# New durations, and a port that two engines share, in the model behind a list scheduler: a two-block transformer kernel on one core

## The chip, the core and the metric

The kernel runs on one core of a Trainium2 chip. A core has five engines with a queue of instructions each, which run in the order in which they were issued: TensorE (PE in the profile, its weight loads PEld) for matrix products, VectorE (DVE), ScalarE (ACT) and GpSimd (POOL) for the rest, SyncE (SP) for issuing transfers. They meet through semaphores alone. The metric is the device time of one execution in microseconds (us).

## The reference

Two transformer blocks over 1024 tokens of width 1024, all in float32. What is cut here is what the argument doesn't touch.

```python
def first_block(x, c, ctx, ...):                # two layers
    for l in range(2):
        sh1, sc1, g1, sh2, sc2, g2 = split(silu(c) @ w_ada[l] + b_ada[l])
        hx = rmsnorm(x, g_pre_mix[l]) * (1 + sc1) + sh1
        q, k, v, u, gv, f = split(hx @ w_in[l])
        y = merge_heads(latent_window_attention(rope(q), rope(k), v, ck, cv, sink[l]),
                        spatial_gating(gelu(u), gelu(gv), ...), fourier_mix(f)) @ w_out[l]
        x = x + g1 * rmsnorm(y, g_post_mix[l])
        hx2 = rmsnorm(x, g_pre_ff[l]) * (1 + sc2) + sh2
        x = x + g2 * rmsnorm(square(relu(hx2 @ w_ff1[l])) @ w_ff2[l], g_post_ff[l])
    return x                                     # layer 0 runs the 256 context tokens too

def second_block(x, c, positions, ...):          # one layer
    h = rms_norm(x, g_mix) * (1 + sc_a) + sh_a
    cq, ckv, kr, dq, dk, dv = split(h @ w_in)
    mixed = concat(mla_attention(...), dilated_attention(...)) @ w_out
    x = x + gt_a * mixed
    h2 = rms_norm(x, g_ffn) * (1 + sc_m) + sh_m
    x = x + gt_m * expert_choice_ffn(h2, ...)    # 16 experts, each takes its 128 best tokens
    return rms_norm(x, g_final)
```

## The kernel before

**Tiling.** The tokens lie in tiles of 128. Matrix products run as two-part float32r products: an operand is split into a rounded high part (a copy) and the low part that is left (a subtraction), and a product is three passes (`mm3`) or two (`mm2`). So each block of weights of 128 x 1024 costs a load, a high copy on ScalarE or VectorE and a low subtraction on VectorE or GpSimd (`split`), and each result that becomes an operand again costs the same (`transpose_split`, `ev`, `expo`).

**What sets the order.** No line of the program says in which order the engines get their work. Each piece of work is a Python generator that yields where another may go ahead (`Task`); `Sched.run` picks, of those that may go on, the one of the best priority, and the instructions that it issues stand behind all earlier ones in their engines' queues. Whether a piece may go on is told by `Model`: a clock for each engine, moved on in `note` by an instruction's estimated cost after its inputs' estimated ends (`POST` and `PRE` are the estimated hand-over between engines). A task that needs an engine is held until that engine's clock is near. `copy`, `add` and `lo_any` also take the engine whose clock says that it will be through first, and `whole` lets a product run as one float32 product, without the split, where VectorE's clock is well behind TensorE's. The costs and clocks are numbers in Python; they set the order and the engine, and no time on the chip.

**Names used below.** The *first seam* is the step from layer 0's feed-forward to layer 1's projections, the *second seam* the one from layer 1's to the second block's. There `ff` ends, `finisher` makes the new residual and the next norm of each tile (`fin0` to `fin7`: `post`, `prenorm`, two times four transposes), and `passes` or `passes2` multiplies the tiles by the next weights (`proj`), which needs the first tile and four blocks of `w_in`, loaded and split by `Weights.task`. At the second seam `tables2` also makes tables of sines and cosines on VectorE. The *latent attention* is `mla_unit`, 16 units of 512 queries of a head: a first product for the maxima, a second for the scores, exponentials on ScalarE (`expo`), sums of them on GpSimd (`acc`), their split, and the product with the values. The *dilated attention* (`dil_unit`, 32 units) may run beside it and runs on behind it.

All engine calls go through `Engine.call`, so every instruction has one line, L186.

```python
    def lo_any(self, out, src, hi):
        n, c = size(out), self.m.clk
        if max(c["POOL"], self.m.now) + n * 0.0022 < max(c["DVE"], self.m.now) + n * 0.00104 + self.lbias:
            self.nc.gpsimd.tensor_sub(out, src, hi.bitcast(F32))
        else:
            self.lo(out, src, hi)
```

Of the kernel before, what the change touches and what calls it, by code (L numbers as in the profile page):

```python
# [38 lines left out]
PRE = 0.14  # L39
# [68 lines left out]
# ---------------------------------------------------------------- the order of the instructions  # L108
class Model:
    """What the instructions issued so far occupy: it decides which piece of work is issued next."""  # L110

    def __init__(self):
        self.clk = dict(PE=0.0, DVE=0.0, ACT=0.0, POOL=0.0, SP=0.0, DMA=0.0)
        self.cell, self.slot, self.last = {}, {}, {}
        self.events = []
        self.now = self.end = 0.0
        self.used = set()
# [11 lines left out]
    POST = dict(PE=0.25, DVE=0.2, ACT=0.15, POOL=0.1)  # L129

    def note(self, eng, cost, outs, ins, dma=False):
# [15 lines left out]
        else:  # L147
            e = self.clk[eng] = t + cost
# [13 lines left out]
def size(ap):  # L162
    n = 1
    for s in ap.shape[1:]:
        n *= s
    return n


class Engine:
# [3 lines left out]
    def __getattr__(self, op):  # L173
        f, m, name = getattr(self._r, op), self._m, self._n

        def call(*a, **k):
# [8 lines left out]
            m.note(eng, cost, outs, ins, "dma" in op)  # L185
# [4 lines left out]
    def cost(self, op, out, ins, k):  # L190
        n = max([size(out)] + [size(i) for i in ins])
# [5 lines left out]
        if e == "PE":  # L197
            if op == "transpose":
                return 0.109 if out.dtype == F32 else 0.056
            n = size(out)  # L200
            if ins[0].dtype == F32:
                return 2 * max(2 * n * 0.000417, 0.107)
            return max(n * 0.000421, 0.107)
        if e == "ACT":
            return 0.06 + n * 0.00083 + (0.09 if k.get("accum_out") is not None else 0)
        ps = any("PSUM" in str(i.space) for i in ins + [out])
        if e == "DVE":
            fast = op in ("tensor_copy", "tensor_scalar", "memset") and not ps and k.get("accum_out") is None
            return 0.07 + n * (0.00052 if fast else 0.00104)
        if op == "tensor_tensor" and k.get("op") == OP.pow:  # L210
            return 0.3 + 0.17 * n
        return 0.1 + n * 0.0022
# [7 lines left out]
class Sched:  # L220
# [16 lines left out]
    def run(self):  # L237
        """until all but the background is done"""
# [55 lines left out]
# ---------------------------------------------------------------- constants of the shapes  # L294
def rnd11(a):
    """float32 rounded to the 11 fraction bits of float32r"""
# [64 lines left out]
# ---------------------------------------------------------------- memory and arithmetic  # L361
class Base:
# [70 lines left out]
    def copy(self, out, src):  # L433
        """on whichever of the two engines is free first"""
# [22 lines left out]
    def mm2(self, out, v, hi, lo, start, stop):  # L457
        """v = [high | low] of 64 columns: the parts of the sum end up in the two halves of the rows"""
# [3 lines left out]
    def whole(self, t):  # L462
        """the vector engine is further behind than the tensor engine: a float32 product rather than two parts"""
# [3 lines left out]
    def fold(self, out, x):  # L467
        """x [high 64 | low 64, tokens] transposed, the halves added"""
# [14 lines left out]
    def bc_row(self, dst, row, n=1024):  # L483
        """every partition gets the row"""
# [16 lines left out]
    def lo_any(self, out, src, hi):  # L501
        """operands on chip: on whichever of the two engines is through first"""
# [7 lines left out]
class Reserve:  # L510
    """blocks kept back for a piece of work that has begun: it can always go on"""
# [32 lines left out]
class Weights:  # L544
    """Blocks of weights in the order of their use: loaded, then split in two float32r parts."""
# [71 lines left out]
class Block1(Base):  # L617
    # ---- start
# [29 lines left out]
    # ---- modulation  # L648
    def mod_pe(self, l, js, room):
        """both vectors of a layer on the tensor engine, 1024 columns at a time"""  # L650
# [33 lines left out]
    def mod_dve(self, l, js, wname, bname, wl, vecs):  # L684
        """weighted rows summed on the vector engine, then over the partitions on the tensor engine: 512 columns at a time"""
# [2722 lines left out]
```

## Time and profile before

| what | value |
|---|---|
| median of three runs | 4331.73 us (4331.38 to 4336.57) |
| span of the profiled execution (first to last instruction) | 4329.5 us |
| TensorE busy in it | 4034.2 us, 93% |
| VectorE, ScalarE, GpSimd busy | 64%, 42%, 18% |
| mean granted TensorE clock | 0.964 |

The profiled execution's own time outside the profiler is not recorded apart from its span; the median of the runs stands 2.2 us above the span. The span is read as TensorE's busy time plus its waits, since it has work or waits for work from the first product to the last. Its busy time is longer than its work, since in some stretches the granted clock is half of the full one.

### The profile page before, as it was taken

Reading aid. Unit: us, or ns where it says so; the run is one execution under the profiler, and the core shown is the slowest. Engines: PE = TensorE matmul, PEld = TensorE weight load, DVE = VectorE, ACT = ScalarE, POOL = GpSimd, SP = SyncE. Lnnn points to the kernel's source line nnn. Section 1 sums busy time; section 2 is a strip of 40 time slices with the busy share of each in tenths; the row PEclk is TensorE's granted clock in tenths of the full one; section 3 lists DMA queues with packets and bytes.
Section 4 is the critical chain, followed back from the end, with each engine's and each line's share of the span. In section 5 each row is a group of like instructions: output and inputs, shape, how many; then the busy total and the mean of one; then the engine's idle time right before and its main releaser. Section 6 shows DMA issues by size and latency. Waiting matters only on the chain. (4 is left out here: it accounts for less than half of the span.)

```text
span 4329.5 us, 54977 instructions
## 1 busy us (share of the span) xinstructions
PE 4034.2 (93%) x19984; PEld 3295.4 (76%) x19984; DVE 2780.2 (64%) x5030; ACT 1825.5 (42%) x3699; POOL 769.1 (18%) x853
## 2 busy tenths in 40 slices
PE   7998999999999979989999999798888898699997
PEld 3777778878887869878888888687676787587776
DVE  6447875666666385777233333814788776888898
ACT  3236643221221233564321222413455653687876
POOL 2111130000000061212000000401567424100001
PEclk8999999999999989999999999899889899799999
DMA  6202322233434240133111112423211345799998
GB/s 220 88 23 79 122 81 89 84 103 118 129 116 126 79 148 22 40 122 112 44 45 44 59 44 81 132 70 95 65 34 30 93 128 195 278 350 369 380 368 304
DMA packets 318761, 552.98 MB, mean 128 GB/s; under 512 B 93117, under 2 KB 177365, under 8 KB 318490
## 3 DMA queue, kind: packets, MB, share of 16 engines
q1 hardware_dynamic: 309130, 515.39, 34.9%
q0 software_dynamic: 9360, 34.08, 2.8%
q8 instruction: 157, 2.57, 0.2%
q14 instruction: 114, 0.93, 0.1%
HBM read 488.42 MB, written 60.97 MB: 127 GB/s over the span
## 5 line engine op out<-in xcount | busy, mean ns | idle before, releaser
L186 PE MATMUL ps<-blk 128*128 128x512 f32 (+3 forms) x16104 | 3542.5, 377 | 84.1 <-DVE blk L186 55.8
L186 PEld LDWEIGHTS ps<-blk 128*128 128x128 f32 (+1 forms) x16104 | 2847.1, 192 | 654.4 <-DVE blk L186 87.6
L186 DVE TENSOR_TENSOR blk<-blk 128x1024 fp32r<-128x1024 f32 (+7 forms) x808 | 922.9, 1182 | 139.1 <-ACT blk L186 126.0
L186 ACT CAST blk<-blk 128x1024 fp32r<-128x1024 f32 (+3 forms) x679 | 661.2, 1022 | 662.3 <-DMA blk<-in_w_ff_dram 390.3
L186 DVE TENSOR_TENSOR blk<-blk,ps 128x512 f32<-128x512 f32 (+1 forms) x488 | 324.8, 675 | 326.5 <-PE ps L186 324.9
L186 ACT CAST blk<-ps 128x512 fp32r<-128x512 f32 (+5 forms) x608 | 275.0, 480 | 441.7 <-PE ps L186 420.9
L186 PE MATMUL ps<-ident,blk 128*128 128x128 f32 (+1 forms) x2024 | 327.9, 296 | 113.6 <-DVE blk L186 53.4
L186 POOL TENSOR_TENSOR blk<-blk 128x1024 f32<-128x1024 f32 (+3 forms) x120 | 252.9, 2113 | 1004.4 <-DMA blk<-in_g_post_ff_dram 647.0
L186 DVE TENSOR_TENSOR blk<-ps,blk 128x512 fp32r<-128x512 f32 (+7 forms) x702 | 349.7, 532 | 108.9 <-ACT blk L186 83.1
L186 PEld LDWEIGHTS ps<-ident,blk 128*128 128x128 f32 x2024 | 261.8, 161 | 178.1 <-ACT blk L186 52.0
L186 ACT ACTIVATE hb<-ps 128x512 f32<-128x512 f32 (+2 forms) x194 | 106.5, 549 | 523.3 <-PE ps L186 512.5
L186 DVE SCALAR_TENSOR_TENSOR hb<-hb,cT 128x512 f32<-128x512 f32 x224 | 164.2, 749 | 112.5 <-DMA hb<-in_w_ada_dram 111.0
L186 ACT ACTIVATE blk<-blk,z 128x256 f32<-128x256 f32 (+2 forms) x406 | 214.4, 532 | 46.3 <-DVE z L186 41.3
L186 DVE CAST blk<-hb 128x512 fp32r<-128x512 f32 (+2 forms) x127 | 48.9, 389 | 262.6 <-ACT hb L186 258.0
L186 ACT ACTIVATE blk<-ps 128x512 f32<-128x512 f32 (+1 forms) x198 | 117.4, 598 | 187.6 <-PE ps L186 182.8
L186 ACT ACTIVATE hb<-hb 128x512 f32<-128x512 f32 (+5 forms) x386 | 176.1, 484 | 37.8 <-DVE hb L186 16.8
L186 ACT ACTIVATE blk<-blk 128x1024 f32<-128x1024 f32 (+4 forms) x157 | 117.4, 751 | 162.7 <-DVE blk L186 141.8
L186 ACT COPY blk<-ps 128x512 f32<-128x512 f32 (+2 forms) x131 | 77.2, 596 | 250.5 <-PE ps L186 250.4
L186 POOL TENSOR_TENSOR hb<-hb,blk 128x512 f32<-128x512 f32 x96 | 170.1, 1771 | 26.6 <-ACT blk L186 20.4
L186 DVE SCALAR_TENSOR_TENSOR blk<-blk,z 128x1024 f32<-128x1024 f32 (+2 forms) x146 | 155.0, 1095 | 21.1 <-POOL z L186 20.3
L186 DVE CAST blk<-ps 128x512 fp32r<-128x512 f32 (+2 forms) x178 | 93.5, 545 | 106.1 <-ACT blk L186 53.3
L186 POOL TENSOR_SCALAR sinkb<-sinkb 128x8 f32<-128x8 f32 x2 | 0.5, 245 | 888.8 <-DMA sinkb<-in_sink_dram 888.8
(150 smaller groups left out, 2060.6 us busy)
## 6 DMA issues: line engine op xcount, KB each, us to landing
blk<-in_w_ff_dram SPq DMA_DIRECT2D x128, 512.0 KB
blk<-in_w_gate_dram SPq DMA_DIRECT2D x128, 512.0 KB
blk<-in_w_up_dram SPq DMA_DIRECT2D x128, 512.0 KB
blk<-in_w_down_dram SPq DMA_DIRECT2D x128, 512.0 KB
hb<-in_w_ada_dram SPq DMA_DIRECT2D x208, 256.0 KB
blk<-in_w_ada_dram SPq DMA_DIRECT2D x40, 512.0 KB
blk<-in_w_in_dram SPq DMA_DIRECT2D x36, 512.0 KB
xd<-blk SPq DMA_DIRECT2D x32, 512.0 KB
```

The costliest lines, as they stand in the source:

```text
L186: return f(*a, **k)
```

## The change

It puts new numbers in `cost`, `POST` and `PRE`, and adds to `Model` the port that VectorE and GpSimd share: an instruction that `shares` marks starts, by the model, after the last marked one of the other engine. All other hunks take out comments and docstrings.

```diff
-PRE = 0.14
+PRE = 0.06
...
         self.cell, self.slot, self.last = {}, {}, {}
+        self.port = dict(DVE=0.0, POOL=0.0)
...
-    POST = dict(PE=0.25, DVE=0.2, ACT=0.15, POOL=0.1)
-
-    def note(self, eng, cost, outs, ins, dma=False):
+    POST = dict(PE=0.25, DVE=0.16, ACT=0.18, POOL=0.12)
+
+    def note(self, eng, cost, outs, ins, dma=False, shared=False):
...
         else:
+            if shared:
+                t = max(t, self.port["DVE" if eng == "POOL" else "POOL"])
+                self.port[eng] = t + cost
             e = self.clk[eng] = t + cost
...
-            m.note(eng, cost, outs, ins, "dma" in op)
+            m.note(eng, cost, outs, ins, "dma" in op, self.shares(op, out, ins))
...
         if e == "PE":
+            n = size(out)
             if op == "transpose":
-                return 0.109 if out.dtype == F32 else 0.056
-            n = size(out)
+                return 0.085 if ins[0].dtype == F32R else 0.112
+            if ins[0].dtype == F32R:
+                return max(n / 2400 + 0.0133, 0.06)
             if ins[0].dtype == F32:
-                return 2 * max(2 * n * 0.000417, 0.107)
-            return max(n * 0.000421, 0.107)
+                return 2 * max(2 * n / 2400 + 0.0025, 0.112)
+            return max(n / 2400 + 0.0025, 0.025)
+        ps = any("PSUM" in str(i.space) for i in ins + [out])
+        acc = k.get("accum_out") is not None
+        column = any(size(i) == 1 for i in ins)
         if e == "ACT":
-            return 0.06 + n * 0.00083 + (0.09 if k.get("accum_out") is not None else 0)
-        ps = any("PSUM" in str(i.space) for i in ins + [out])
+            return (0.06 if ps else 0.1) + n * 0.00083 + (0.1 if acc else 0) + (0.075 if column else 0)
         if e == "DVE":
-            fast = op in ("tensor_copy", "tensor_scalar", "memset") and not ps and k.get("accum_out") is None
-            return 0.07 + n * (0.00052 if fast else 0.00104)
+            fast = op in ("tensor_copy", "tensor_scalar", "memset") and not ps and not acc
+            return 0.07 + n * (0.00052 if fast else 0.00104) + (0.062 if op == "scalar_tensor_tensor" or fast and column else 0)
         if op == "tensor_tensor" and k.get("op") == OP.pow:
-            return 0.3 + 0.17 * n
-        return 0.1 + n * 0.0022
+            return 0.25 + 0.19 * n
+        return 0.2 + n * 0.0021
+
+    def shares(self, op, out, ins):
+
+        n = sum("PSUM" not in str(i.space) and size(i) > 1 for i in ins)
+        if self._n == "POOL":
+            return n > 0
+        return self._n == "DVE" and (n > 1 or n == 1 and op in ("tensor_copy", "tensor_scalar") and "PSUM" not in str(out.space))
```

The work is the same but for what the three choosers decide. Over the whole program VectorE issues 3 instructions more and ScalarE 29 fewer; GpSimd gets 7 more tensor-tensor instructions, among them 9 low parts of exponentials, 5 of queries and 3 of keys in the latent attention, all VectorE's before. In the dilated attention 19 products more run as one float32 product (13 of 256 columns, 6 of 128) in place of 38 float32r ones, and in the first block's attention 7 of 512 columns in place of 14.

The order changes all along the program. These are the places that the prediction speaks of. In each pair, the first rows are of before (L186) and the second of the change (L190).

At the second seam, TensorE's queue: `ident` marks the finisher's transposes, the long rows of `blk` alone are first the last of `ff` (multiples of 12 up to 24) and then `proj`.

```order
L186 MATMUL ps<-blk 128x512 x12
L186 MATMUL ps<-ident,blk 128x128 x4
L186 MATMUL ps<-blk 128x512 x24
L186 MATMUL ps<-ident,blk 128x128 x20
L186 MATMUL ps<-blk 128x512 x60
L186 MATMUL ps<-ident,blk 128x128 x4
```

```order
L190 MATMUL ps<-blk 128x512 x12
L190 MATMUL ps<-ident,blk 128x128 x4
L190 MATMUL ps<-blk 128x512 x12
L190 MATMUL ps<-ident,blk 128x128 x16
L190 MATMUL ps<-blk 128x512 x90
L190 MATMUL ps<-ident,blk 128x128 x4
L190 MATMUL ps<-blk 128x512 x30
L190 MATMUL ps<-ident,blk 128x128 x4
```

Before, the last rows of `ff` are followed by 20 transposes (of `fin4`, `fin5`, again both, and the first half of `fin6`) and then `proj`; now `proj` comes after 16 transposes, with 90 products ahead of the second half of `fin5` and 120 ahead of the first of `fin6`.

At the same place, SyncE's queue: `xd_93` is the finisher's store of a tile's residual, `in_w_in` a block of the next weights, `posi` and `inv` inputs of the tables.

```order
L186 DMA xd_93<-blk 128x1024
L186 DMA posi<-in_positions_dram 128x8x1
L186 DMA hb<-in_inv_dram 128x96
L186 DMA blk<-in_w_in_dram 128x2x512
L186 DMA xd_93<-blk 128x1024
L186 DMA blk<-in_w_in_dram 128x2x512 x2
L186 DMA blk<-in_positions_dram 128x1024
L186 DMA invT<-in_invT_dram 128x2
L186 DMA blk<-in_w_in_dram 128x2x512 x3
```

```order
L190 DMA xd_93<-blk 128x1024 x2
L190 DMA posi<-in_positions_dram 128x8x1
L190 DMA hb<-in_inv_dram 128x96
L190 DMA blk<-in_w_in_dram 128x2x512 x6
L190 DMA blk<-in_positions_dram 128x1024
L190 DMA invT<-in_invT_dram 128x2
L190 DMA xd_93<-blk 128x1024
```

Before, one block of weights stands ahead of the store of `fin6` and the fourth behind it and behind the inputs of the tables; now six stand together ahead of that store.

At the first seam, SyncE's queue: `xd_91` is the residual's store (in the first rows of `fin5`, `fin6` and `fin7` in turn, in the second of `fin4`, `fin5` and `fin6`; `xd_90` is a tile that is read).

```order
L186 DMA xd_91<-blk 128x1024
L186 DMA blk<-in_w_in_dram 128x2x512 x3
L186 DMA xd_91<-blk 128x1024
L186 DMA blk<-in_w_in_dram 128x2x512
L186 DMA xd_91<-blk 128x1024
L186 DMA blk<-in_w_in_dram 128x4x256 x4
```

```order
L190 DMA blk<-xd_90 128x1024
L190 DMA blk<-in_w_in_dram 128x2x512 x2
L190 DMA xd_91<-blk 128x1024
L190 DMA blk<-in_w_in_dram 128x2x512
L190 DMA xd_91<-blk 128x1024
L190 DMA blk<-in_w_in_dram 128x2x512
L190 DMA xd_91<-blk 128x1024
```

Before, three blocks of weights stand behind the store of `fin5` and the fourth behind that of `fin6`; now the fourth stands behind the store of `fin5`. On TensorE the first 12 products of `proj` stood behind all eight transposes of `fin5` and now stand ahead of them.

In the latent attention, GpSimd's queue: `hb<-blk` and `hb<-hb,blk` are the sums of exponentials (one unit has one and six), `MEMSET` belongs to the queries.

```order
L186 MEMSET blk 1x512
L186 TENSOR_TENSOR hb<-hb 32x512
L186 TENSOR_TENSOR blk<-hb,blk 96x512
L186 TENSOR_TENSOR hb<-blk 128x512
L186 TENSOR_TENSOR hb<-hb,blk 128x512 x6
```

```order
L190 TENSOR_TENSOR hb<-hb 32x512
L190 TENSOR_TENSOR hb<-blk 128x512
L190 TENSOR_TENSOR blk<-hb,blk 96x512
L190 TENSOR_TENSOR hb<-hb,blk 128x512 x6
L190 TENSOR_TENSOR blk<-blk 128x1024
```

Before, a unit's sums follow each other and no low part of 128 x 1024 is among them; now GpSimd also has such a subtraction (`blk<-blk 128x1024`) behind or between a unit's sums, at nine places of the stage.

## Rows read from the trace of the kernel before

**Rows 1.** The page: span, and busy time, share and instructions of each engine

```profile
span 4329.5 us, 54977 instructions
...
PE 4034.2 (93%) x19984; PEld 3295.4 (76%) x19984; DVE 2780.2 (64%) x5030; ACT 1825.5 (42%) x3699; POOL 769.1 (18%) x853
```

**Rows 2.** Stretches: length; PE, PEld, DVE, ACT, POOL busy (x); clock, DMA, GB/s

```profile
1554.00:1613.00 59.00, 36.64 (x169) 29.75 (x168) 58.56 (x61) 22.74 (x45) 45.34 (x42) 0.83 0.47 160
2100.00:2700.00 600.00, 600.00 (x2649) 496.81 (x2648) 189.29 (x255) 133.97 (x187) 2.40 (x1) 1.00 0.18 55
2709.00:2790.00 81.00, 54.30 (x247) 44.15 (x247) 75.05 (x102) 33.12 (x61) 43.78 (x40) 0.85 0.40 129
3020.00:3397.00 377.00, 319.75 (x1463) 251.46 (x1463) 304.53 (x443) 205.50 (x371) 243.12 (x152) 0.89 0.17 43
3400.00:3567.00 167.00, 156.11 (x1033) 141.25 (x1033) 135.82 (x396) 108.30 (x299) 50.38 (x28) 0.94 0.47 124
3800.00:4300.00 500.00, 489.13 (x2290) 395.07 (x2288) 447.41 (x479) 388.29 (x501) 37.85 (x25) 1.00 0.97 362
```

**Rows 3.** What TensorE waited for, whole span: us in total, times, longest

```profile
PE ps L186 <- DVE blk L186: 112.4, 82, 14.7
```

**Rows 4.** Timeline of the second seam: start, us, instruction, idle before

```profile
2745.99 0.40 SPq L186 DMA_DIRECT2D blk<-in_w_in_dram  x1
...
2752.79 0.33 SPq L186 DMA_DIRECT2D xd<-blk  x1
2753.28 1.19 SPq L186 DMA_DIRECT2D blk<-in_w_in_dram  x2
...
2755.66 13.35 SPq L186 DMA_DIRECT2D blk<-in_w_in_dram  x3
...
2756.31 2.82 PE L186 MATMUL ps<-ident,blk 128*128 128x128 f32 x12 [7.44 <-DVE blk L186]
...
2766.66 5.88 POOL L186 TENSOR_TENSOR blk<-blk 128x1024 f32<-128x1024 f32 x1 [8.34 <-DVE blk L186]
2767.39 2.36 DVE L186 TENSOR_TENSOR blk<-blk 128x1024 fp32r<-128x1024 f32 x2
...
2772.60 1.11 PE L186 MATMUL ps<-ident,blk 128*128 128x128 f32 x4 [13.47 <-POOL blk L186]
...
2773.36 16.09 PE L186 MATMUL ps<-blk 128*128 128x512 f32 x60
```

**Rows 5.** Timeline of the first seam

```profile
1592.68 1.83 SPq L186 DMA_DIRECT2D blk<-in_w_in_dram  x3
...
1598.69 0.34 SPq L186 DMA_DIRECT2D xd<-blk  x1
...
1599.14 0.37 SPq L186 DMA_DIRECT2D blk<-in_w_in_dram  x1
...
1604.56 3.48 DVE L186 TENSOR_TENSOR blk<-blk 128x1024 fp32r<-128x1024 f32 x3
...
1606.96 1.97 PE L186 MATMUL ps<-ident,blk 128*128 128x128 f32 x8 [14.66 <-DVE blk L186]
...
1608.58 4.03 PE L186 MATMUL ps<-blk 128*128 128x512 f32 x12
```

**Rows 6.** Timeline of the end of layer 0 attention

```profile
508.43 1.94 PE L186 MATMUL ps<-ident,blk 128*128 128x128 f32 x8 [3.92 <-DVE blk L186]
```

**Rows 7.** Groups of instructions: a plain float32 product of 512 columns

```profile
L186 PE MATMUL ps<-blk,cT 128*2 128x512 f32 x128 | 62.3, 623 | 6.3 <-DMA blk<-in_w_ada_dram 6.3
```

**Rows 8.** VectorE in 2100 to 2700 us, where GpSimd is idle

```profile
L186 DVE TENSOR_TENSOR blk<-blk 128x1024 fp32r<-128x1024 f32 x54 | 64.9, 1223 | 56.2 <-ACT blk L186 56.2
```

**Rows 9.** The latent attention, 3020 to 3397 us

```profile
L186 POOL TENSOR_TENSOR hb<-hb,blk 128x512 f32<-128x512 f32 x96 | 170.1, 1771 | 26.6 <-ACT blk L186 20.4
L186 DVE TENSOR_TENSOR blk<-blk 128x1024 fp32r<-128x1024 f32 x67 | 112.6, 1685 | 9.9 <-ACT blk L186 9.4
```

**Rows 10.** GpSimd over the whole span: its low parts of 128 x 1024

```profile
L186 POOL TENSOR_TENSOR blk<-blk 128x1024 fp32r<-128x1024 f32 x17 | 41.8, 2465 | 39.9 <-ACT blk L186 28.4 <-PE ps L186 8.9 <-DVE rden L186 1.5
```

## The prediction

> **What bounds the kernel now.** The page first: TensorE is busy for 4034 of the 4329.5 us of the span [rows 1]. With 93% on one engine, no order of the same products can give more than the waits that are left and what the low clock adds, so the question is where the waits lie. The table by stretches tells that. In the feed-forward TensorE waits for nothing (600 of 600 us), and in the experts it is busy for 489 of 500 us while the transfer engines are at 0.97: there a new order has nothing to win. It waits at the two seams (22 of 59 us at the first, 27 of 81 at the second) and in the latent attention (57 of 377 us), all with a granted clock of 0.83 to 0.89, where 1.00 is 2.4 GHz and the low level 1.2 [rows 2]. The table of waits says for whom: VectorE's blocks end 112 us of them [rows 3]. So I cost the change at those three places, and the float32 products that it adds by themselves.
>
> **Second seam: -11 us.** Before, `proj` starts at 2773.36, right behind the first transposes of `fin6`, for which TensorE waited 13.47 us: an addition on GpSimd that began at 2766.66 and took 5.88. Ahead of that lies a wait of 7.44 us for `fin5` and `fin4` [rows 4]. Now `proj` stands ahead of `fin6`, so what it waits for is its own: the fourth block of weights. Its load is the first of the three at 2755.66, and its low part is the first of the two from 2767.39, done at about 2768.6 (half of 2.36 us). So with the old loads `proj` could have begun 4.8 us sooner. But the loads move too: the blocks behind the first waited in SyncE's queue for the store of `fin6` at 2752.79, and now six stand ahead of it. At the pace of two in 1.19 us the fourth is issued some 2 us behind the first, at about 2748 in place of 2755.7, so 8 us sooner. Its low part now stands behind fewer instructions on VectorE as well: five low parts follow each other there, where before three were followed by a tile's transposes, its norm and a table, and then two. I take 6.6 of the 8 us on top of the 4.8: `proj` starts at about 2762. What is late next is `fin6`: it has 120 products ahead of it, 27 us at 0.2265 us each (600 us by 2649 [rows 2]), which reach to 2789, and its transposes were ready at 2772.6 before. Bounds: -4 (the order alone) and -13.5 (the whole wait); the 7.44 us stay.
>
> **First seam: -5 us.** Here `proj` starts at 1608.58, and the low part of its fourth block ends at 1608.04 (1604.56 and 3.48). So the wait of 14.66 us that is booked on `fin5` hides a wait for weights, and putting `proj` ahead of `fin5` alone gives nothing. The fourth load went out at 1599.14, right behind the store of `fin6` at 1598.69; now it stands behind the store of `fin5`, with which before the three loads from 1592.68 went out [rows 5]. At 0.6 us each that is about 1594.5, 4.6 us sooner, and `fin6` and `fin7` no longer stand ahead on VectorE. Bounds: 0 and -14.7.
>
> **End of layer 0's attention: -3 us.** The transposes of `front1` waited 3.92 us with nothing behind them [rows 6]; they now stand ahead of the last attention products, which fill the wait. Bounds: 0 and -3.9. In layer 1 the same is done to a shorter wait; I give it nothing.
>
> **Float32 products: +5 us.** The nearest row is a float32 product of 512 columns with two rows out: 128 records for 64 products, 62.3 us, so 0.97 us each [rows 7]. Two float32r products are 0.45 us, so 0.52 us more, and by the columns an estimated 0.26 at 256 and 0.13 at 128: 7 x 0.52 + 13 x 0.26 + 6 x 0.13 = 7.8 us of TensorE. Most are in the dilated attention, where TensorE is busy for 156 of 167 us [rows 2], so little is hidden; but each saves VectorE a split there. +5, bounds 0 and +7.8.
>
> **Latent attention: -5 us.** The port is plain in the rows: VectorE's subtraction of 128 x 1024 takes 1.223 us where GpSimd is idle [rows 8] and 1.685 us here, where GpSimd is busy for 243 of 377 us, 96 of its additions at 1.771 us each [rows 9]. The 67 of them lose 31 us that way, which the old model didn't count: it issued work that was not to be ready. Now four more units of the dilated attention (12 in place of 8) are through before the last latent unit, products that wait for nothing of this stage, and nine low parts of exponentials leave VectorE (9 x 1.685 = 15 us) for GpSimd, where one takes 2.465 us [rows 10], 22 us in all. VectorE at 304 of 377 us and GpSimd at 243 [rows 2] both have room, but a low part on GpSimd stands behind sums in its queue. I take a small gain, -5, with bounds of -28 (half of TensorE's 57 us) and +39 (below).
>
> A rule stands against this term: the Trainium skill, page "Perfetto Trace Analysis", section "Optimizing Scalar/DVE Operations", says that moving work between GpSimd and VectorE might not help, since they share a read port. By it the nine low parts free nothing and hold the port for longer, 9 x (2.465 - 1.223) = +11 us in place of -5; it gives the second rival below.
>
> **Everything else: 0.** The order changes in every stage, but the feed-forward has no waits to lose, pieces of attention and Fourier work only change places, and the routing is the same instructions on VectorE.
>
> Sum: -11 - 5 - 3 + 5 - 5 = -19, so a span of 4310.5 us. The profiled execution has 4329.5, and the median of the runs stands 2.2 us above it: **4313 us**.
>
> **Rivals.** *Slower: GpSimd is late in the latent attention.* Each of the nine low parts ends up to 2.465 + 2 x 1.771 - 1.685 = 4.3 us later than on VectorE, behind two sums, and the product with the values waits for it in TensorE's queue with all that stands behind: up to 39 us. For it speaks that TensorE's waits here are for VectorE most of all; against it that more dilated products stand between. It decides from 24 us on (the other terms are -14, and 10 more pass the measure); at three quarters, 29 us, the time is 4313 + 5 + 29 = 4347. *No change: the port eats the gain.* With +11 in the latent attention, as above, the sum is -11 - 5 - 3 + 5 + 11 = -3, 4329 us. For it speaks that both engines lose time to the port now; against it that VectorE's wait falls as well as GpSimd's rises. *Faster still:* half of the latent attention's 57 us go, -28 in place of -5: 4290 us. For it speaks that the old model was blind to the port just there; against it that VectorE has little spare time.
>
> **How the numbers follow.** The forecast 0.48, slower 0.20, no change 0.17, faster still 0.15. A measurement of this kernel tells about 0.2%, 8.7 us, from no change (4323 to 4340). Nearly all of the forecast's own range (4300 to 4328) and all of the last case are faster: 0.60. The rest of the forecast and most of the second rival are the same: 0.20. Slower: 0.20. The range leaves out the lower half of the last case and the upper half of the first rival: 4285 to 4345; the forecast's own is 4300 to 4328.
>
> **What would show it.** At the second seam the row with 60 products should be one with 90, starting some 11 us sooner by the end of `ff`, with no wait of 13 us ahead of it; at the first seam a wait of 9 to 10 us in place of 14.66. In the latent attention, a busy GpSimd above 0.65 of the stage, VectorE's subtractions still near 1.7 us, and TensorE's waits at 50 us or so. The experts should take the same time from their first product on. The prediction is wrong if waits appear where there are none now, in the attention of the first block above all, if TensorE's waits for GpSimd's blocks grow from stage to stage, or if the 57 us grow.

## The result: slower by 1.0%

The changed kernel takes 4380.66 us (median of 4 runs, 4375.11 to 4384.74), the kernel before 4334.15 beside it (4331.38 to 4343.10): ratio 1.0100, interval [1.0087, 1.0114]. The forecast was 4313, and the range ended at 4345. The profiled execution took 4380.09, its span is 4378.3.

The page answers to [rows 1]: TensorE is busy for 30 us more and the span is 49 us longer, so it waits 19 us more and also takes 30 us longer for its products, on the same number of records, at a mean granted clock of 0.959 (0.964 before).

```profile
span 4378.3 us, 54861 instructions
...
PE 4063.8 (93%) x19984; PEld 3315.3 (76%) x19984; DVE 2744.7 (63%) x5033; ACT 1827.5 (42%) x3662; POOL 791.1 (18%) x860
```

The table by stretches answers to [rows 2]: first seam, second seam, latent attention, experts.

```profile
1558.00:1617.00 59.00, 43.61 (x210) 35.27 (x210) 58.85 (x63) 24.75 (x52) 41.61 (x44) 0.88 0.40 134
2727.00:2808.00 81.00, 69.02 (x311) 55.94 (x310) 71.72 (x93) 34.84 (x68) 44.27 (x46) 0.92 0.39 132
...
3040.00:3449.00 409.00, 350.22 (x1648) 278.22 (x1646) 285.90 (x461) 237.43 (x438) 265.11 (x170) 0.89 0.18 43
3830.00:4330.00 500.00, 470.62 (x2208) 386.36 (x2207) 428.80 (x463) 377.85 (x492) 59.58 (x25) 0.97 0.97 358
```

Both seams gained, as forecast: 7 and 15 us more work in stretches of the same length. The experts, where TensorE was busy for 489 of 500 us, now have 471. The table of waits over the whole span says for whom; VectorE's row [rows 3] fell by half, and others grew, the gathered blocks of the experts (3.7 us before) most plainly:

```profile
PE ps L190 <- ACT blk L190: 64.0, 101, 3.6
PE ps L190 <- DVE blk L190: 58.3, 68, 3.3
PE ps L190 <- DVE hb L190: 44.8, 18, 22.7
PE ps L190 <- POOL blk L190: 42.4, 16, 12.6
PE ps L190 <- DMA blk<-h,idxT: 30.4, 7, 7.7
```

TensorE has the same number of records under the same names in both programs (a float32 product counts as two), so each stage can be timed from the start of its first product to that of the next stage's first. In us, from the two profiled executions:

| | stage | before | after | change |
|-|-|-|-|-|
| A | start, layer 0's attention and output projection | 639.6 | 654.7 | +15.1 |
| B | first feed-forward, seam, projections to the last key | 1074.9 | 1062.8 | -12.1 |
| C | layer 1's attention, with queries and Fourier work | 213.8 | 243.9 | +30.1 |
| D | output projection | 103.3 | 102.9 | -0.4 |
| E | second feed-forward and seam | 878.3 | 864.3 | -14.0 |
| F | rest of the projections, latent and dilated attention, output, routing | 806.5 | 814.5 | +7.9 |
| G | experts | 576.5 | 599.2 | +22.6 |
| H | final sum | 10.7 | 9.3 | -1.4 |

The sum is +47.8. The gains (B and E, 26 us) are larger than the 16 forecast; the losses lie in A, C and G, for which the forecast had -3 and twice zero, and in F (-5 and +5). By the table by stretches over each stage, TensorE's waiting changed by +2.5 us in A, -8.1 in B, +17.0 in C, -12.7 in E, +0.6 in F and +20.1 in G; the rest of each change is longer or shorter busy time. Stage A before and after, and in a third kernel that has the order of the kernel before on every engine up to the experts (`late_gather`, below):

```profile
5.09:644.67 639.58, 583.93 (x3086) 442.81 (x3086) 414.57 (x993) 282.87 (x825) 127.68 (x233) 0.97 0.30 103
5.12:659.78 654.66, 596.52 (x3085) 449.80 (x3085) 417.90 (x1004) 281.17 (x811) 117.59 (x228) 0.95 0.29 101
5.20:653.90 648.70, 590.46 (x3086) 448.18 (x3086) 415.80 (x993) 283.20 (x825) 125.07 (x233) 0.96 0.30 101
```

The first and the third row differ by 9 us with the same order, 6.5 of them busy time, so of A's 15 us as little as 6 may be the change's.

**The seams.** The timeline answers to [rows 4]. TensorE's waits ahead of the row of `proj` are 5.74 and 3.97 us in place of 7.44 and 13.47, and the row has 90 products:

```profile
2768.58 9.18 SPq L190 DMA_DIRECT2D xd<-blk  x2
2779.49 4.01 SPq L190 DMA_DIRECT2D blk<-in_w_in_dram  x6
...
2782.26 1.12 PE L190 MATMUL ps<-ident,blk 128*128 128x128 f32 x4 [5.74 <-POOL blk L190]
2787.35 1.97 PE L190 MATMUL ps<-ident,blk 128*128 128x128 f32 x8 [3.97 <-POOL blk L190]
2788.96 22.36 PE L190 MATMUL ps<-blk 128*128 128x512 f32 x90
...
2790.83 5.76 DVE L190 TENSOR_TENSOR blk<-blk 128x1024 fp32r<-128x1024 f32 x5
```

The last feed-forward product ends at 2775.9 here and at 2748.4 before, so `proj` begins 13 us behind it, where it was 25. It begins while five of the six low parts of its weights are still to be made (the last row), right behind the transposes. At the first seam the wait is 12.60 in place of 14.66 [rows 5]; 6 us of B's gain lie in smaller waits, most of them ahead of it, and 4 in shorter busy time:

```profile
1607.86 1.97 PE L190 MATMUL ps<-ident,blk 128*128 128x128 f32 x8 [12.60 <-POOL blk L190]
1609.48 3.86 PE L190 MATMUL ps<-blk 128*128 128x512 f32 x12
```

**The experts.** On GpSimd's queue, before, from the eighth expert on each gather is issued some 9.5 us behind a scatter and 24 to 27 us ahead of its transposes:

```profile
3960.64 1.59 POOL L186 DMA_INDIRECT xo<-blk,idxT  x1 [24.63 <-DVE blk L186]
3970.19 0.98 POOL L186 DMA_INDIRECT blk<-h,idxT  x1 [7.97 <-ACT blk L186]
3997.18 1.59 POOL L186 DMA_INDIRECT xo<-blk,idxT  x1 [26.00 <-DVE blk L186]
4006.73 0.98 POOL L186 DMA_INDIRECT blk<-h,idxT  x1 [7.97 <-DMA blk<-in_w_gate_dram]
```

After, gathers come in no rhythm, and TensorE stands in front of their transposes:

```profile
4071.80 1.72 POOL L190 DMA_INDIRECT blk<-h,idxT  x1 [0.30 <-PE ps L190]
4078.15 1.12 PE L190 MATMUL ps<-ident,blk 128*128 128x128 f32 x4 [4.81 <-DMA blk<-h,idxT]
...
4112.03 1.22 POOL L190 DMA_INDIRECT blk<-h,idxT  x1 [5.94 <-ACT blk L190]
4120.39 1.12 PE L190 MATMUL ps<-ident,blk 128*128 128x128 f32 x4 [6.75 <-DMA blk<-h,idxT]
```

From a gather's issue to its first transpose, experts 3 to 15, worked out from such rows: before 18.8 to 28.5 us and no wait; after 7.2, 8.0, 12.6, 10.2, 17.3, 10.8, 29.5, 6.3, 8.4, 14.9, 5.6, 9.0 and 16.6. Six of these waited; for them (5.6 to 10.2) it is the time that the block took to arrive.

**Layer 1's attention.** In the order of the program before, the 124 products of its Fourier work stand between attention products almost to the end. After, they stand in one piece of some 40 us (1795 to 1834), together with the last queries; the attention from the third tile on comes behind it, alone. The stage before and then after:

```profile
1719.50:1933.40 213.90, 197.60 (x1230) 169.78 (x1227) 171.15 (x520) 132.24 (x407) 43.47 (x95) 0.98 0.25 82
```

```profile
1722.60:1966.50 243.90, 210.61 (x1228) 172.64 (x1227) 175.87 (x537) 130.53 (x389) 43.55 (x97) 0.96 0.21 72
```

TensorE waits for 33 us in this stage where it waited for 16, and is busy for 13 us longer at a granted clock of 0.96 in place of 0.98.

### The profile page after: what moved, and what is told of

Read it like the earlier page. It is cut to its first block, busy times and chain, and to the rows that moved or that the text cites. A ratio compares the mean times of both kernels' runs of the same rounds, so it can differ in the third digit from the quotient of the medians.

```text
span 4378.3 us, 54861 instructions
## 1 busy us (share of the span) xinstructions
PE 4063.8 (93%) x19984; PEld 3315.3 (76%) x19984; DVE 2744.7 (63%) x5033; ACT 1827.5 (42%) x3662; POOL 791.1 (18%) x860
## 5 line engine op out<-in xcount | busy, mean ns | idle before, releaser
L190 PE MATMUL ps<-blk 128*128 128x512 f32 (+6 forms) x16104 | 3556.6, 379 | 87.4 <-DVE blk L190 38.9
L190 PEld LDWEIGHTS ps<-blk 128*128 128x128 f32 (+2 forms) x16104 | 2862.3, 193 | 657.2 <-DVE blk L190 62.8
L190 DVE TENSOR_TENSOR blk<-blk 128x1024 fp32r<-128x1024 f32 (+8 forms) x806 | 909.1, 1167 | 237.9 <-ACT blk L190 228.0
L190 ACT CAST blk<-blk 128x1024 fp32r<-128x1024 f32 (+3 forms) x696 | 678.0, 1021 | 665.3 <-DMA blk<-in_w_ff_dram 365.7
L190 DVE TENSOR_TENSOR blk<-blk,ps 128x512 f32<-128x512 f32 (+1 forms) x488 | 322.7, 676 | 316.8 <-PE ps L190 315.8
L190 ACT CAST blk<-ps 128x512 fp32r<-128x512 f32 (+4 forms) x553 | 256.6, 487 | 531.6 <-PE ps L190 505.7
L190 POOL TENSOR_TENSOR blk<-blk 128x1024 f32<-128x1024 f32 (+4 forms) x122 | 261.6, 2150 | 966.8 <-PE ps L190 667.9
L190 PE MATMUL ps<-ident,blk 128*128 128x128 f32 (+1 forms) x2024 | 329.0, 296 | 106.9 <-POOL blk L190 32.5
L190 DVE TENSOR_TENSOR blk<-ps,blk 128x512 fp32r<-128x512 f32 (+7 forms) x687 | 340.9, 530 | 120.6 <-ACT blk L190 100.9
L190 PEld LDWEIGHTS ps<-ident,blk 128*128 128x128 f32 x2024 | 261.6, 160 | 178.7 <-ACT blk L190 55.9
L190 ACT ACTIVATE hb<-ps 128x512 f32<-128x512 f32 (+2 forms) x194 | 106.6, 549 | 524.5 <-PE ps L190 512.4
L190 DVE SCALAR_TENSOR_TENSOR hb<-hb,cT 128x512 f32<-128x512 f32 x224 | 165.5, 754 | 127.0 <-DMA hb<-in_w_ada_dram 125.5
L190 DVE CAST blk<-hb 128x512 fp32r<-128x512 f32 (+2 forms) x129 | 51.6, 402 | 282.5 <-ACT hb L190 278.0
L190 ACT ACTIVATE blk<-blk,z 128x256 f32<-128x256 f32 (+2 forms) x406 | 214.3, 532 | 32.1 <-DVE z L190 31.9
L190 ACT COPY blk<-ps 128x512 f32<-128x512 f32 (+2 forms) x155 | 91.9, 603 | 269.8 <-PE ps L190 269.3
L190 DVE CAST blk<-ps 128x512 fp32r<-128x512 f32 (+2 forms) x218 | 108.9, 515 | 136.5 <-ACT blk L190 70.1
L190 ACT ACTIVATE hb<-hb 128x512 f32<-128x512 f32 (+3 forms) x378 | 174.1, 488 | 24.8 <-DVE blk L190 9.5
L190 ACT ACTIVATE blk<-ps 128x512 f32<-128x512 f32 (+1 forms) x198 | 116.9, 599 | 157.5 <-PE ps L190 152.1
L190 ACT ACTIVATE blk<-blk 128x1024 f32<-128x1024 f32 (+4 forms) x157 | 117.4, 751 | 149.8 <-DVE blk L190 136.6
L190 DVE SCALAR_TENSOR_TENSOR blk<-blk,z 128x1024 f32<-128x1024 f32 (+2 forms) x146 | 158.8, 1120 | 18.6 <-POOL z L190 18.5
L190 POOL TENSOR_TENSOR hb<-hb,blk 128x512 f32<-128x512 f32 x96 | 156.5, 1632 | 33.3 <-ACT blk L190 28.0
L190 POOL TENSOR_SCALAR sinkb<-sinkb 128x8 f32<-128x8 f32 x2 | 0.5, 246 | 885.1 <-DMA sinkb<-in_sink_dram 885.1
```

Source lines behind the costliest of these rows:

```text
L190: return f(*a, **k)
```

## The experiments

Theory from these rows: the losses are separate accidents of order, each in its place: a gather that is issued late, Fourier work that is not there when the attention waits, and something at the end of layer 0's attention. Main rival: the port in the model, or a slower chain of VectorE, ScalarE and GpSimd, costs in all stages alike. The gaps of a gather "in the model's time" in the expectations are between its issue and its transposes by the scheduler's own clock. The numbers by stage against before, from one profiled execution each (ahead of the first difference in order, stage A differed by up to 9 us between executions, the others by 4, so less is not read):

| kernel | A | B | C | E | F | G | ratio to before |
|-|-|-|-|-|-|-|-|
| after | +15 | -12 | +30 | -14 | +8 | +23 | 1.0100 [1.0087, 1.0114] |
| `act_only` | +1 | 0 | -5 | -2 | +9 | +4 | 0.9996 [0.9986, 1.0005] |
| `late_fourier` | +15 | -10 | +3 | -14 | +6 | +20 | 1.0045 [1.0028, 1.0062] |
| `early_gather` | +15 | -10 | +30 | -16 | +6 | +4 | 1.0060 [1.0038, 1.0083] |
| `no_port` | +11 | -3 | -5 | -1 | -2 | +50 | 1.0123 [1.0106, 1.0139] |
| `both` | +13 | -9 | +3 | -14 | +9 | +8 | 1.0026 [1.0016, 1.0035] |
| `port_only` | +9 | -7 | +4 | -11 | +37 | +3 | 1.0072 [1.0056, 1.0089] |
| `three` | +6 | -9 | +3 | -14 | +13 | +3 | 0.9996 [0.9987, 1.0006] |
| `no_whole` | +7 | -9 | +10 | -14 | +31 | +3 | 1.0055 [1.0038, 1.0072] |
| `port_at_seams` | +13 | -7 | +11 | -11 | -1 | 0 | 1.0004 [0.9994, 1.0013] |
| `port_between` | +6 | -12 | +3 | -14 | +1 | +6 | 0.9964 [0.9950, 0.9977] |
| `old_pre` | +7 | -9 | +25 | -16 | +30 | +19 | 1.0116 [1.0101, 1.0132] |
| `tail_port` | +15 | -1 | -1 | -2 | +1 | 0 | 1.0036 [1.0026, 1.0045] |
| `packed_fourier` | +7 | +1 | +23 | -4 | +1 | +2 | 1.0039 [1.0025, 1.0053] |
| `late_gather` | +9 | -2 | 0 | -2 | -1 | +72 | 1.0160 [1.0143, 1.0177] |
| `port_from_out` | -3 | -9 | +4 | -12 | +2 | 0 | 0.9955 [0.9938, 0.9971] |

**`late_fourier`**, from the changed kernel:

```diff
-yield lambda: ... (S.ctx or len(S.xT) <= FLIM)
+yield lambda: ... (S.ctx or len(S.xT) <= (0 if self.fstage else FLIM))
```

> The changed kernel, in which the Fourier work of layer 1 may not begin before all eight query tiles are projected; the rest has the same rules. Theory (layer 1's attention loses because all the Fourier products are issued in one piece ahead of the attention, which then has nothing to fill its waits): the 33 us of that stage come back, 4348 (4340 to 4356), and the stage's waits of TensorE fall from 33 to some 16 us. Rival (the attention's own chain of VectorE, ScalarE and GpSimd has become slower by its new order, with or without filler): 4 us or less come back, 4376 or more.

4352.73 us, 28 less than the changed kernel, all of it in C (+3 in place of +30), with 15 us of waits there. The rival falls.

**`early_gather`**, from the changed kernel:

```diff
-self.s.spawn(gather(1), 3, "gather1")
+self.s.spawn(gather(1), 1, "gather1")
...
-self.s.spawn(gather(e + 2), 3, f"gather{e + 2}")
+self.s.spawn(gather(e + 2), 1, f"gather{e + 2}")
```

> The changed kernel, with the gathers of the experts at priority 1 in place of 3, ahead of the splitting of weights (2); nothing ahead of the experts changes. Theory (a gather issued only 5 to 8 us of the model's time ahead of its transposes is late, since its transfer takes longer than that): TensorE's waits for gathered blocks fall from 30 us to 10 or less and the time by 15 to 20, 4361 to 4366. Rival (the transfer engines at 0.93 set the experts' pace, and the wait only changes its place): the time stays within 4 us of the changed kernel, 4377 or more, and the waits turn up for blocks of weights.

4359.92 us, 21 less; the experts are 4 us from before, the waits for gathered blocks 14.4 us. Three gathers whose transposes came 9.5 to 10.6 us behind the issue still waited 3 to 4 us of that, the ten with 14 us or more did not. The transfer engines are no bound that gives the wait back.

**`act_only`**, the kernel before with one line of the new durations:

```diff
-return 0.06 + n * 0.00083 + (0.09 if accum_out ... else 0)
+return (0.06 if ps else 0.1) + n * 0.00083 + (0.1 if acc else 0) + (0.075 if column else 0)
```

> The kernel before with ScalarE's new durations alone; all other numbers of the model are the old ones, and there is no port. Theory (the experts lose because the gathers' turn is issued later, and ScalarE's durations decide that): the experts take about 15 to 20 us more, with waits of TensorE for the gathered block of 15 us or more in all (3.7 before); the other stages within some 10 us, so 4345 to 4360. Rival (the port is what costs, everywhere): without the port nothing is lost, 4334, and the experts' waits for the gathered block stay near 4 us.

4335.16 us: no change, which is the rival's time, and the experts +4. (The profiled execution, the slowest of ten, took 4340.) The size was wrong: ten of the thirteen gathers were still issued 12 us or more ahead, and the other three waited 5.5 us in all, so ScalarE's durations move them but not far enough to cost much.

**`no_port`**, from the changed kernel:

```diff
-m.note(eng, cost, outs, ins, "dma" in op, self.shares(op, out, ins))
+m.note(eng, cost, outs, ins, "dma" in op)
```

> The changed kernel without the port, with all of its durations. Theory (two accidents of order, of which the port is needed for the one in layer 1's attention and not for the one in the experts): the Fourier products of layer 1 are spread again and that stage gives back 15 to 33 us, while the experts keep their waits of 20 us or more for gathered blocks: 4348 to 4366. Rival (the port is the cause of all of it): 4310 to 4334 with no waits for gathered blocks. Second rival (the port is harmless, the durations do it): 4375 to 4385.

4388.47 us, no better than the changed kernel and above all three bounds. C is back (-5), but the experts are +50: eight of the thirteen gathers waited, and the row of waits has 48 us. So the port isn't the cause of the late gathers. The loss in C needs it, though: with the port and the old durations (`port_only`, below) C is +4, without the port and with the new durations -5, and the Fourier work stands in one piece only with the two together. And without the port E's gain is gone (-1 in place of -14).

**`both`**, the edits of `late_fourier` and `early_gather`:

> The changed kernel with both edits: the Fourier work of layer 1 after the eighth query tile, and the gathers at priority 1. Theory (two losses in two places that have nothing to do with each other): they add, 4380.7 - 28 - 21 = 4332 (4326 to 4338), the time of the kernel before. Rival (one gain makes the other smaller, since the transfers or the clock set the pace behind): 4342 or more.

4342.26 us: 38 of the 49 us, outside my bounds and at the edge of the rival's. C keeps its whole gain (+3); the experts stood at +8 in this execution and F at +9, with the same 14 us of waits for gathered blocks, so where the other 11 us went is not shown.

**`port_only`**, the kernel before with this alone:

```diff
+self.port = dict(DVE=0.0, POOL=0.0)
...
+if shared:
+    t = max(t, self.port["DVE" if eng == "POOL" else "POOL"])
+    self.port[eng] = t + cost
...
+def shares(self, op, out, ins):
...
```

> The kernel before with the shared port alone in its model, all durations the old ones. Theory (the port moves fin5 and fin6 behind the projection at the second seam and makes layer 0's attention slower; ScalarE's durations make the gathers late): the second seam gives 7 to 9 us, layer 0's attention loses 8 to 16, layer 1's attention keeps its spread Fourier work and the experts their early gathers: 4325 to 4345, and 4 us or so of waits for gathered blocks. Rival (the port by itself is what hurts attention and experts): 4360 or more.

4364.42 us, outside my bounds. The experts and layer 1's attention are as expected, E gives 11 us; F loses 37, which I had not expected. The rival was right on the time, though not on the stages.

**`three`**, as `both`, with the port from the end of layer 0's attention on:

```diff
+self.own = False
...
-if shared:
+if shared and self.own:
...
 yield lambda: X.attd
+self.m.own = True
```

> As the kernel with both edits, and the model knows the port only from the end of layer 0's attention on. Theory (the 16 us that layer 0's attention lost come by the port in the model): that stage gives 10 to 14 us back, 4318 to 4322, faster than the kernel before by 0.3%. Rival (that stage lost by the durations, or by chance): 4330 or more.

4330.74 us, within its interval the time of before, and at the edge of the rival's bounds: 12 us less than `both`, as the theory says, but from a higher start. A fell from +13 to +6, little beside what it differs by itself, so this run doesn't decide (`tail_port` does).

**`no_whole`**, as `both`, with the float32 products switched off:

```diff
-FT = 2.0
-FD = 2.0
+FT = 1000.0
+FD = 1000.0
```

> As the kernel with both edits, and no product is made in float32 for VectorE's sake: 9 of 512 columns in the attention, 13 of 256 and 6 of 128 in the dilated attention become two float32r products with a split on VectorE. Theory of the prediction (each costs TensorE 0.52, 0.26 or 0.13 us that little hides): 4 to 8 us faster than with both edits, 4325 or so. Rival (each saves a split on an engine for which TensorE waits there, so it pays): the same or slower by up to 15 us, most of it in the latent and dilated attention.

4356.91 us, 15 slower than `both`, 22 in F and 7 in C: the rival. The float32 products pay for themselves here (the order around them changes too, so this is the price of the choice, not of one product).

**`port_at_seams`**, the kernel before with the port on from `attd` of either layer to the end of the projections behind it:

> The kernel before with all its old durations; its model knows the port only from the end of an attention to the end of the projections behind it (so over both feed-forwards and both seams), nowhere else. Theory (the seams gain by the port in the model, and every loss lies in the stages that this leaves as they were): end of the first attention to the first seam -8 to -12, second feed-forward and second seam -9 to -14, the rest within 6: 4310 to 4320, faster than the kernel before by 0.3 to 0.5%. Rival (an order that differs at the seams upsets the attention and the latent attention behind them by as much): 4330 or more.

4334.83 us, outside my bounds and within the rival's: the gains came (B -7, E -11), but A lost 13 and C 11. Its order is the old one up to the last units of layer 0's attention. `attd` is set when the last units are started and not when they are done: the port was on for them.

**`port_between`**, as `three`, with the port off again behind the second block's projections:

> The changed kernel with the late Fourier work and the early gathers, and the port in its model from the end of layer 0's attention to the end of the second block's projections: not in the latent and dilated attention. Theory (the 8 to 10 us that these stages lost come with the port): latent and dilated attention with what follows are within 4 us of the kernel before, 4316 to 4326. Rival (they come from the durations, or the order is as good either way): 4330 or more.

4320.68 us, faster than before by 0.36%. F is +1 in place of `three`'s +13: there the port costs.

**`old_pre`**, the changed kernel with `PRE = 0.14`:

> The changed kernel with PRE back at 0.14 (how long after its operand the model lets TensorE begin). Theory (this number only shifts the order by accident): the Fourier work of layer 1 stays in one piece (+30 there), but from the ninth expert on the gathers are issued 30 us or more of the model's time ahead, so the waits for gathered blocks fall from 30 to some 18 us: 4366 to 4376. Rival (a smaller number is what makes TensorE's order too tight everywhere): 4345 or less.

4388.03 us, neither. The waits for gathered blocks fell to 10.2 us and C kept its loss, but F lost 22 more: with the new durations the smaller number helps the latent attention.

**`tail_port`**, the kernel before with the port on from `attd` of layer 0 to its first output projection:

> The kernel before, with its old durations; its model knows the port only from the moment when the last units of layer 0's attention are started to the first output projection. Theory (the port reorders these last units, and that is the loss at this place): from att6.1 to the output projection 10 to 14 us more at a lower granted clock, all else as before: 4344 to 4350. Rival (the loss came from elsewhere in the stage): 4331 to 4338.

4349.01 us, 13.5 more than the kernel before, in the profiled execution all in A. TensorE's timeline at the end of that attention has a wait of 3.22 us that was not there, some smaller ones, and the wait of [rows 6] grown from 3.92 to 5.53 us:

```profile
498.43 3.92 PE L191 MATMUL ps<-ident,blk 128*128 128x128 f32 x12 [3.22 <-ACT blk L191]
...
515.52 1.10 PE L191 MATMUL ps<-ident,hb 128*128 128x64 f32 x8 [0.68 <-ACT hb L191]
522.15 1.94 PE L191 MATMUL ps<-ident,blk 128*128 128x128 f32 x8 [5.53 <-DVE blk L191]
```

and the stretch has this busy time and granted clock, here and then before:

```profile
480.00:526.00 46.00, 33.48 (x169) 25.27 (x169) 33.66 (x83) 32.55 (x88) 4.90 (x13) 0.81 0.30 92
```

```profile
480.00:512.00 32.00, 26.70 (x165) 21.58 (x164) 29.80 (x81) 27.39 (x83) 4.82 (x13) 0.95 0.41 136
```

169 products in 33.5 us against 165 in 26.7: half of the 14 us is waiting, half nearly the same work at the lower clock. VectorE and ScalarE have nearly the same instructions (83 and 88 against 81 and 83).

**`packed_fourier`**, the kernel before, in which only this is added to the start of an attention unit:

```diff
 self.room(...) and self.roomh(1)
+and (self.fstage == 0 or t < 2 or S.fourd)
```

> The kernel before, in which attention units from the third tile on wait in layer 1 until the Fourier work is issued, so that it stands in one piece ahead of them, as in the changed kernel. Theory (without that filler the attention's waits lie open): layer 1's attention takes 20 to 33 us more, 4355 to 4368. Rival (it was the new order inside the attention): 10 us or less, 4336 to 4345.

4353.61 us, 18 more, just under my bounds; C +23. All but 7 us of the stage's loss is made by the order of the Fourier work alone, with the old model.

**`late_gather`**, the kernel before with one line ahead of a gather's transfer:

```diff
+yield lambda: self.sn >= e - 2
 x = self.blk()
 nc.gpsimd.indirect_dma_start(out=x, ...
```

> The kernel before, in which the gather of each expert from the fourth on is issued only behind the scatter of the expert three ahead, as in the changed kernel: 8 us of the model's time ahead of its transposes in place of 20 to 28. Theory (a gather takes longer than that to land, and TensorE waits for its block): 3 to 4 us for each of 13, the experts 30 to 50 us longer, 4365 to 4385. Rival (the transfer engines set the experts' pace anyway): 4345 or less.

4407.35 us, 72 more, all in G and above what I had expected. The transposes of all thirteen came 8.8 to 12.8 us behind the issue, and all waited, 56 us in all. These gathers stand 1.9 to 2.9 us behind a scatter and took 8.6 to 12.8 us to land, where the same thirteen took 5.3 to 9.4 before, so the run shows that a late gather costs, and more than the changed kernel's order does (+23). TensorE's row of waits, and one gather with its transposes:

```profile
PE ps L190 <- DMA blk<-h,idxT: 59.3, 14, 6.4
...
4027.22 1.36 POOL L190 DMA_INDIRECT blk<-h,idxT  x1 [0.30 <-PE ps L190]
...
4037.71 1.08 PE L190 MATMUL ps<-ident,blk 128*128 128x128 f32 x4 [5.32 <-DMA blk<-h,idxT]
```

**`port_from_out`**, the kernel before with the port on from layer 0's first output projection to the end of the second block's projections:

```diff
 hi, lo = zT.pop(i)
+self.m.own = True
...
 yield from self.passes2(X, self.W2)
+self.m.own = False
```

> The kernel before, with its old durations; its model knows the port from layer 0's first output projection to the end of the second block's projections. Theory (with the end of layer 0's attention left alone, only the gain at the seams is left, less some 5 to 11 us in layer 1's attention, whose Fourier work now starts earlier): 4316 to 4326. Rival (the gain at the seams is given back again): 4330 or more.

4316.08 us, faster than before by 0.45%, [0.9938, 0.9971], and the best of all: old durations, and the port only where it helps.

## Why the prediction was wrong

- **Second seam, -11: right in sum, wrong in two steps.** E is -14, with the two waits 11.2 us shorter. But the loads did not move as I had it: the fourth goes out 5 us behind the last feed-forward product, where it was 7 us behind, not 8 us sooner. And `proj` did not wait for its fourth block: it began right behind transposes that wait for GpSimd, with five of six low parts still to be made. The gain is that the transposes of `fin6`, with their wait of 13.47 us, no longer stand ahead of it; those of the tiles ahead of `fin6` wait 9.7 us in place of 7.4. That the sum fits is in part luck. `port_only` has the gain (-11) and `no_port` hasn't (-1): it comes by the port.
- **First seam, -5: too small.** B is -12. The wait that I costed gave 2.1; smaller waits gave 6, and shorter busy time 4. I had looked at one row of a stretch with 22 us of waits.
- **End of layer 0's attention, -3: the sign was wrong.** I moved `front1` into its wait and costed nothing for what was moved behind it. A is +15 in this execution, of which some 6 to 15 us are the change's; `tail_port` makes 13.5 (median of ten runs) in the kernel before by the order of the last units alone: they end later, with nothing behind them to fill TensorE, and it runs at the lower clock.
- **Float32 products, +5: the wrong question.** By the columns they cost TensorE 7.8 us, of which I kept 5, but leaving them out costs 15 (`no_whole`). They are chosen when VectorE is behind; that their split is what would then be waited for is likely, and not shown apart from the new order.
- **Latent attention, -5: F is +8.** Not by the first rival's mechanism: waits for GpSimd are 9 us here (7 before). The two stretches of latent and dilated attention, output and routing are, before and then after:

```profile
3010.00:3601.00 591.00, 516.64 (x2689) 427.88 (x2689) 457.69 (x870) 323.66 (x687) 306.46 (x190) 0.90 0.28 76
3601.00:3716.00 115.00, 79.26 (x461) 68.15 (x461) 90.88 (x312) 37.71 (x78) 47.51 (x37) 0.83 0.63 230
```

```profile
3027.00:3628.00 601.00, 527.26 (x2689) 436.44 (x2688) 415.33 (x830) 339.79 (x707) 320.78 (x205) 0.89 0.28 75
3628.00:3741.00 113.00, 77.33 (x460) 66.72 (x458) 83.64 (x308) 37.45 (x79) 43.09 (x35) 0.83 0.65 237
```

  VectorE is relieved of 50 us (548.6 to 499.0), and TensorE's idle time stays: 110.1 and 109.4 us. Its busy time grows by 8.7 us, of which the float32 products explain about 4 by the columns. The subtractions of [rows 9] became slower, the additions faster:

```profile
L190 POOL TENSOR_TENSOR hb<-hb,blk 128x512 f32<-128x512 f32 x96 | 156.5, 1632 | 33.3 <-ACT blk L190 28.0
```

```profile
L190 DVE TENSOR_TENSOR blk<-blk 128x1024 fp32r<-128x1024 f32 x60 | 108.7, 1817 | 48.0 <-ACT blk L190 44.2 <-POOL blk L190 2.5 <-DMA hb<-mq 1.2
```

  The Trainium skill, page "Perfetto Trace Analysis", section "Optimizing Scalar/DVE Operations", says that moving work between GpSimd and VectorE might not help. The trace agrees in so far as VectorE's 50 us bought TensorE nothing; it is no clean test, since the nine low parts are some 15 of the 50 us and ScalarE is 16 us busier. What costs is a model that knows the port in this stage: `port_between` against `three` 13 us of F, `port_only` against `port_from_out` 35, and the changed kernel against `no_port` 10. Durations alone can do it too (`act_only` has +9 without a port, in its slowest execution). Which of the reordered pieces does it was not tried.
- **"Everything else: 0": the step that failed.** "Pieces of attention and Fourier work only change places" cost C 30 us; `late_fourier` gets 27 of it back and `packed_fourier` makes 23 in the kernel before. In the experts "a new order has nothing to win", but it had 23 us to lose: `early_gather` gets 19 back, `late_gather` makes 72. Which task comes first decides both (in layer 1 the Fourier work and an attention unit both ask for ten free blocks, as the code has it). The late gathers need only the new durations: without the port they cost more still (+50). The packed Fourier work needs the port and the new durations together: it is gone in `no_port` (-5) and in `port_only` (+4). And apart from the float32 products no term stood for longer busy time, which is 30 of the 49 us, 13 of them in C and 13 in A. The prediction had named the sign itself, waits in the attention of the first block where there were none, and given it no chance of its own.

The rivals of the forecast were all about the latent attention; none stood where 68 us were lost. The slower one had the right side by luck: its mechanism could have cost 39 us, and the rows have 2 us more of waits for GpSimd.

What stays open: which single duration, beside the port, lets the Fourier work go first, which makes the gathers late (ScalarE's alone costs 4 us), which piece costs in F, and why C in `port_at_seams` lost 11.

## What to carry to other kernels

A stage in which nothing waits has nothing to win by a new order, and the more to lose: ask of each transfer and each filler there how far ahead it is issued, and forecast what happens if that lead shrinks. When a scheduler's numbers change, read the whole new order for such leads (gather to use, filler to the waits it fills, the last units of a stage) before pricing the places that wait now. And a model that knows more does not by itself make a better order: each stage can fall one way or the other, so switch such a change on stage by stage. Here the port alone, with the old durations, made the kernel 0.45% faster where it was on from layer 0's output projection to the second block's projections, and 0.72% slower where it was on everywhere.

## What the hardware showed that was not expected

- A gather of 128 rows of 4 KB took 5.6 to 12.8 us from its issue to the product that waited for it, beside the experts' weight traffic (the 19 that waited in the changed kernel and in `late_gather`); the model has 3.5 us for it, before and after.
- Waits at the end of a stage can cost twice: in `tail_port` 169 products took 33.5 us at a granted clock of 0.81 over the stretch, where 165 took 26.7 at 0.95.
- With the same order on every engine, the first stage took 639.6 to 648.7 us in different profiled executions (before and `late_gather`): TensorE was busy for 583.9 and 590.5 us of it, at a mean granted clock of 0.97 and 0.96.
